# Gate and up projections by Strassen's seven products, with middle sums in PSUM

## The chip, the cores and the metric

The kernel runs on one core of a Trainium2 chip. The metric is device time in microseconds (us) of one execution. Engines are named as the profile names them: PE (TensorE, matrix products; PEld is its weight load), DVE (VectorE), ACT (ScalarE), POOL (GpSimd) and SP (SyncE, which issues DMAs).

## The reference

Two residual layers on x of 512 tokens by 1024 channels, float32. Layer 0 mixes tokens by chunked retention, layer 1 by stick-breaking attention. Each is followed by a feed-forward block, which is what the change is about:

```
h = rms_norm(x, ffn_norm)
gate, up = split(h @ w_in, 2)          # w_in: 1024 x 5632
x = x + (silu(gate) * up) @ w_out      # w_out: 2816 x 1024
```

## The kernel before

Everything is kept with channels on the partitions and the 512 tokens along the free dimension, so x is 8 tiles (k) of 128 channels by 512 tokens, and the 2816 hidden channels are 22 tiles (f).

**Float32 by three products.** PE works on float32r operands. Every operand is split in a high part and the float32r rest: weights by `Weights` (high `wh`, ACT, L72; rest `wl`, DVE, L73), activations by `to_pair`. `split3` (L131 to L133) then makes three matmuls for one product: high by high, high by low, low by high. Every matmul has its own weight load.

**Weights.** Each load is 128 by 1024 floats (512 KB), issued by SP in the order of use (L55), three ahead, in a ring of three `raw` buffers; the split is two ahead, in rings of three. One such item feeds 24 matmuls.

**Feed-forward** (`s_ffn`), once a layer:
- The norm's factor per token (`row`) comes late, from `stats_col` and `stats_row`, so the products run on x with the norm's gain only (`xh`, `xl`), and `ffn_act` multiplies gate and up by `row`.
- `ffn_first`: gate and up of f = 0, 1 in four banks, two k tiles a step, while the last tiles of x are finished.
- `ffn_tile(f)`: 24 matmuls of 512 columns for gate, 24 for up, a PSUM bank each. Then `ffn_act`: gate times `row` (L502, DVE), silu (L504, ACT), up times `row` (L506, DVE), product (L507, DVE), split into `hh` (L138, ACT) and `hl` (L139, DVE).
- After f = 10 and after f = 21 `ffn_out_chunk` multiplies the 11 hidden tiles by w_out, two output tiles at a time, and `add_x` (L233, DVE) adds the bank to x. The last output tile of the kernel is cut in two token halves of 256 columns, so that its first half leaves early; its adds are L526.

PSUM has eight banks in one ring (tag `mm`). The program is written as a list of steps; within an engine, the order of instructions that the queues finally hold is set at build time by a planner that takes the first instruction in program order whose operands it reckons ready. On the chip each engine runs its queue in that order and waits on semaphores.

Of the kernel before, what the change touches and what calls it, by code (L numbers as in the profile page):

```python
# [17 lines left out]
P = 128  # L18
# [8 lines left out]
HALF = FF // P // 2  # L27


class Weights:  # L30
    """Weights in the order of their use: loaded ahead, and split into a float32r
    part and the float32r rest, whose sum is the float32 weight."""

    def __init__(self, nc, raw, split, load_ahead, split_ahead):
        self.nc, self.raw, self.split = nc, raw, split
        self.aps, self.raws, self.parts = [], {}, {}
        self.n_load = self.n_split = self.n_take = 0
        self.load_ahead, self.split_ahead = load_ahead, split_ahead
        self.hooks = {}
        self.first = None  # per half of the first load: what to load before it, what to do before its split  # L40

    def load(self, n):
        nc = self.nc
        while self.n_load < min(n + self.load_ahead, len(self.aps)):
            for hook in self.hooks.pop(self.n_load, ()):
                hook()
            ap = self.aps[self.n_load]
            t = self.raw.tile([P, 1024], F32, tag="raw", name=f"raw{self.n_load}")
            w = ap.shape[-1]
            if self.n_load == 0 and self.first:  # L50
                for half, (ready, _) in zip((slice(0, w // 2), slice(w // 2, w)), self.first):
                    ready()
                    nc.sync.dma_start(t[:, half], ap[:, half])
            else:
                nc.sync.dma_start(t[:, :w], ap)  # L55
            self.raws[self.n_load] = (t, w)
            self.n_load += 1

    def advance(self, n):
        nc = self.nc  # L60
        self.load(n)
        while self.n_split < min(n + self.split_ahead, self.n_load):
            t, w = self.raws.pop(self.n_split)
            h = self.split.tile([P, 1024], F32R, tag="wh", name=f"wh{self.n_split}")
            l = self.split.tile([P, 1024], F32R, tag="wl", name=f"wl{self.n_split}")
            parts = [slice(0, w)]
            if self.n_split == 0 and self.first:
                parts = [slice(0, w // 2), slice(w // 2, w)]
            for i, part in enumerate(parts):
                if len(parts) > 1:  # L70
                    self.first[i][1]()
                nc.scalar.activation(h[:, part], t[:, part], AF.Copy)  # L72
                nc.vector.tensor_tensor(l[:, part], t[:, part], h[:, part].bitcast(F32), ALU.subtract)  # L73
            self.parts[self.n_split] = (h, l, w)
            self.n_split += 1

    def take(self):
        n = self.n_take
        self.advance(n + 1)
        self.n_take += 1  # L80
        return self.parts.pop(n)
# [3 lines left out]
def trunk(ctx, tc, x_in, gains_in, ret_tok, ret_ch, ret_o, sb_in, sb_o4, sb_o2, ffn_in2, ffn_in, ffn_out,  # L85
          cos_in, sin_in, decay_in, out):
    nc = tc.nc
    cp = ctx.enter_context(tc.tile_pool(name="cp", bufs=1))
    xp = ctx.enter_context(tc.tile_pool(name="xp", bufs=1))
    xgp = ctx.enter_context(tc.tile_pool(name="xgp", bufs=8))  # L90
    raw = ctx.enter_context(tc.tile_pool(name="raw", bufs=3))
    split = ctx.enter_context(tc.tile_pool(name="split", bufs=3))
    st = ctx.enter_context(tc.tile_pool(name="st", bufs=2))
    W = Weights(nc, raw, split, 3, 2)
    psr = ctx.enter_context(tc.tile_pool(name="psr", bufs=8, space=bass.MemoryType.PSUM))

    # gains: columns 0-15 mixer (layer, k), 16-31 ffn, 32-47 retention output, 48 q, 49 k
# [22 lines left out]
    zero = cp.tile([P, P], F32, name="zero")  # L120
    nc.vector.memset(zero, 0.0)
    start = psr.tile([P, S], F32, tag="mm", name="start")
# [5 lines left out]
    def split3(ps, a, b, start, stop):  # L128
        """(ah + al) b's three leading products; a and b are (high, low) pairs."""
# [5 lines left out]
    def to_pair(h, l, src, scale=None):  # L135
        """h + l = src * scale, both float32r."""
# [7 lines left out]
    def norm_in(k, gcol):  # L144
        """x[k] with the norm's gain (the norm's factor per token comes later), and its squares."""
# [35 lines left out]
    def tok_chunk(c, banks, kks=(0, 1)):  # L181
        """A quarter of [512 tokens, 512 outputs]: two k tiles."""
# [12 lines left out]
    def ch_tile(bank):  # L195
        """[128 outputs, 512 tokens]"""
# [6 lines left out]
    def ch_chunk(c, banks):  # L203
        """A quarter of four times [128 outputs, 512 tokens]: two k tiles."""
# [42 lines left out]
    def run():  # L247
        W.aps = list(order)
        W.hooks = load_hooks
        W.n_load = W.n_split = W.n_take = 0  # L250
        for fn in steps:
            fn()
        assert W.n_take == len(order)
        order.clear()
        steps.clear()

# [13 lines left out]

    def psum():
        return psr.tile([P, S], F32, tag="mm", name="mm")
# [19 lines left out]
    def rope_tables():  # L292
        # the norm's factor per token goes with the rotation
# [176 lines left out]
    ff = {}  # L470

    def ffn_open():
        ff["ctx"] = ExitStack()
        ff["p"] = ff["ctx"].enter_context(tc.tile_pool(name="ffp", bufs=HALF + 2))
        ff["t"] = ff["ctx"].enter_context(tc.tile_pool(name="fft", bufs=2))

    def ffn_first(c):
        def go():
            if c == 0:
                ff["first"] = [psum() for _ in range(4)]  # L480
            ch_chunk(c, ff["first"])
            if c == 3:
                stats_col(psum)
        return go

    def ffn_tile(f):
        def go():
            gate, up = psum(), psum()
            ch_tile(gate)
            if f == 2:  # L490
                stats_row(psum, ff["t"])
                ffn_act(0, *ff["first"][0:2])
            ch_tile(up)
            if f == 2:
                ffn_act(1, *ff["first"][2:4])
            ffn_act(f, gate, up)
        return go

    def ffn_act(f, gate, up):
        row = state["row"]  # L500
        gs = ff["t"].tile([P, S], F32, tag="gs", name="gs")
        nc.vector.tensor_tensor(gs, gate, row, ALU.mult)  # L502
        sil = ff["t"].tile([P, S], F32, tag="sil", name="sil")
        nc.scalar.activation(sil, gs, AF.Silu)  # L504
        us = ff["t"].tile([P, S], F32, tag="us", name="us")
        nc.vector.tensor_tensor(us, up, row, ALU.mult)  # L506
        nc.vector.tensor_tensor(us, us, sil, ALU.mult)  # L507
        h = ff["p"].tile([P, S], F32R, tag="hh", name="hh")
        l = ff["p"].tile([P, S], F32R, tag="hl", name="hl")
        to_pair(h, l, us)  # L510
        ff["hid"][f] = (h, l)

    def ffn_out_chunk(half, mp, c, gcol, to):
        cuts = [slice(0, S // 2), slice(S // 2, S)] if half == 1 and mp == 3 and to is out else []

        def go():
            if c == 0:
                ff["banks"] = [psum() for _ in range(2 + (len(cuts) > 0))]
            ks = list(range(4 * c, min(4 * c + 4, HALF)))
            out_chunk(ff["banks"], [ff["hid"][half * HALF + k] for k in ks], c == 0, c == 2, cuts=cuts)  # L520
            if c == 2:
                for m in range(2):
                    if cuts and m == 1:
                        for bank, cut in zip(ff["banks"][1:], cuts):
                            part = x[KT - 1][:, cut]
                            nc.vector.tensor_tensor(part, bank[:, : S // 2], part, ALU.add)  # L526
                            nc.sync.dma_start(to[KT - 1][:, cut], part)
                    elif half == 0:
                        add_x(2 * mp + m, ff["banks"][m], None)
                    else:  # L530
                        add_x(2 * mp + m, ff["banks"][m], gcol, to)
        return go

    def s_ffn(layer, gcol, to):
        step(ffn_open)
        ff["hid"] = {}
        for half in range(2):
            if half == 0:
                for c in range(4):
                    step(ffn_first(c), ffn_in2[layer, c])  # L540
            for f in range(2 if half == 0 else HALF, (half + 1) * HALF):
                step(ffn_tile(f), ffn_in[layer, f], ffn_in[layer, 2 * HALF + f])
            for mp in range(4):
                for c in range(3):
                    w = ffn_out[layer, half, mp][:, 1024 * c : min(1024 * (c + 1), 256 * HALF)]
                    step(ffn_out_chunk(half, mp, c, gcol, to), w)
        step(lambda: ff["ctx"].close())
# [347 lines left out]
```

## Time and profile before

| | |
|---|---|
| median of 3 runs | 1412.11 us (1411.46 to 1412.31) |
| span of the profiled execution, first to last instruction | 1412.2 us |
| PE busy | 1400.5 us, 99% |
| DVE, ACT, POOL busy | 736.5, 512.4, 205.8 us |
| bytes moved by DMA | 130.57 MB, 92 GB/s |

The profiled execution's span and the median of the runs are the same to 0.1 us, so times of the trace can be set against the median as they stand. "Busy" PE is a sum over overlapping matmuls; how fast PE goes is read from the distance between the starts of two matmuls.

### The profile page before, as it was taken

The page shows a single profiled execution, that of the slowest core. Times are in us where ns is not written, and L with a number is a line of the kernel's source. Part 1 is how long each engine was busy: PE and PEld are TensorE (multiplying, and loading weights), DVE is VectorE, ACT ScalarE, POOL GpSimd, SP SyncE. Part 2 cuts the span into 40 slices and gives each one's busy share as a digit, 9 for nine tenths or more (in the row PEclk, how much of TensorE's full clock was granted, in tenths as well). Part 3 has the DMA queues.
Part 4 walks back from the last instruction along what each step waited for, and adds up shares of the span by engine and source line. Part 5 has one row for each costly group of instructions (what it writes and reads, how often), then busy time and mean ns, then how long its engine had stood idle before and what let it go on. Part 6 is the DMA issues. An engine that isn't in the chain of part 4 may idle for free.

```text
span 1412.2 us, 16105 instructions
## 1 busy us (share of the span) xinstructions
PE 1400.5 (99%) x6331; PEld 1148.8 (81%) x6331; DVE 736.5 (52%) x947; ACT 512.4 (36%) x768; POOL 205.8 (15%) x262
## 2 busy tenths in 40 slices
PE   9999999999999999999999999999999999999999
PEld 7888888888888888888888877777788888888887
DVE  6555355364374443344434367889994443344432
ACT  5333233232353232223233356657653232223221
POOL 3000000000020000000002245677740000000000
PEclk9999999999999999999999999999999999999999
DMA  6332322213222323332334222122113323333232
GB/s 224 94 93 76 96 75 86 94 60 104 75 90 90 104 87 97 101 102 92 92 106 148 87 90 75 46 60 90 46 60 105 97 94 97 101 95 99 89 109 71
DMA packets 39388, 130.57 MB, mean 92 GB/s; under 512 B 4496, under 2 KB 4752, under 8 KB 39312
## 3 DMA queue, kind: packets, MB, share of 16 engines
q1 hardware_dynamic: 39312, 129.54, 29.6%
q8 instruction: 49, 0.80, 0.2%
q14 instruction: 27, 0.22, 0.0%
HBM read 125.33 MB, written 4.19 MB: 92 GB/s over the span
## 4 chain that ended last, share of the span: by engine, by line
PE 88%; DVE 4%; POOL 4%; issue 3%; ACT 1%; DMA 0%; POOLq 0%; SPq 0%; DVEq 0%; ACTq 0%
PE mm L131 29%; PE mm L133 29%; PE mm L132 28%; POOL w L667 1%; DVE sn L666 1%; POOL sn L660 1%; POOL w L660 1%; POOL qf L603 1%; PE mm L405 0%; DVE kk L636 0%; DVE wtl L139 0%; PE mm L701 0%; DVE wl L73 0%; PE mm L653 0%; PE mm L652 0%
## 5 line engine op out<-in xcount | busy, mean ns | idle before, releaser
L72 ACT ACTIVATE wh<-raw 128x1024 fp32r<-128x1024 f32 (+2 forms) x233 | 243.0, 1043 | 708.8 <-PE mm L132 413.2
L73 DVE TENSOR_TENSOR wl<-raw,wh 128x1024 fp32r<-128x1024 f32 (+2 forms) x233 | 286.2, 1229 | 276.6 <-ACT wh L72 275.5
L131 PE MATMUL mm<-xh,wh 128*128 128x512 f32 x832 | 324.5, 390 | 0.0
L133 PE MATMUL mm<-xh,wl 128*128 128x512 f32 x832 | 323.9, 389 | 0.0
L132 PE MATMUL mm<-xl,wh 128*128 128x512 f32 x832 | 323.8, 389 | 0.0
L132 PEld LDWEIGHTS mm<-xl,wh 128*128 128x128 f32 x832 | 156.2, 188 | 32.6
L133 PEld LDWEIGHTS mm<-xh,wl 128*128 128x128 f32 x832 | 156.2, 188 | 32.5
L131 PEld LDWEIGHTS mm<-xh,wh 128*128 128x128 f32 x832 | 156.2, 188 | 32.1
L132 PE MATMUL mm<-wl,xh 128*128 128x512 f32 x448 | 176.5, 394 | 1.9 <-DVE wl L73 1.9
L131 PE MATMUL mm<-wh,xh 128*128 128x512 f32 x448 | 176.8, 397 | 0.2 <-ACT wh L72 0.2
L133 PE MATMUL mm<-wh,xl 128*128 128x512 f32 x448 | 176.2, 393 | 0.0
L131 PE MATMUL mm<-hh,wh 128*128 128x512 f32 (+1 forms) x363 | 140.6, 387 | 0.0
L133 PE MATMUL mm<-hh,wl 128*128 128x512 f32 (+1 forms) x363 | 139.8, 385 | 0.0
L132 PE MATMUL mm<-hl,wh 128*128 128x512 f32 (+1 forms) x363 | 138.6, 382 | 0.0
L132 PEld LDWEIGHTS mm<-wl,xh 128*128 128x128 f32 x448 | 84.7, 189 | 20.0 <-DVE wl L73 2.6
L131 PEld LDWEIGHTS mm<-wh,xh 128*128 128x128 f32 x448 | 84.5, 189 | 19.6 <-issue 1.7
L158 POOL TENSOR_TENSOR sq<-sq,sqt 128x512 f32<-128x512 f32 x28 | 42.8, 1528 | 390.6 <-issue 293.9
L133 PEld LDWEIGHTS mm<-wh,xl 128*128 128x128 f32 x448 | 84.7, 189 | 18.1 <-issue 0.2
L506 DVE TENSOR_TENSOR us<-mm,row 128x512 f32<-128x512 f32 x44 | 30.4, 690 | 125.2 <-PE mm L133 125.2
L233 DVE TENSOR_TENSOR x<-mm,x 128x512 f32<-128x512 f32 x87 | 59.4, 686 | 57.6 <-PE mm L133 57.5
L133 PEld LDWEIGHTS mm<-hh,wl 128*128 128x128 f32 x363 | 68.1, 188 | 15.0
L132 PEld LDWEIGHTS mm<-hl,wh 128*128 128x128 f32 x363 | 68.1, 188 | 14.3
(115 smaller groups left out, 1608.2 us busy)
## 6 DMA issues: line engine op xcount, KB each, us to landing
raw<-in_ffn_in_dram SPq DMA_DIRECT2D x88, 512.0 KB, 3.5
raw<-in_ffn_out_dram SPq DMA_DIRECT2D x32, 512.0 KB, 3.6
raw<-in_ret_tok_dram SPq DMA_DIRECT2D x31, 512.0 KB, 3.6
raw<-in_sb_in_dram SPq DMA_DIRECT2D x24, 512.0 KB, 3.5
raw<-in_ret_ch_dram SPq DMA_DIRECT2D x16, 512.0 KB, 3.5
raw<-in_ret_o_dram SPq DMA_DIRECT2D x16, 512.0 KB, 3.5
raw<-in_ffn_out_dram SPq DMA_DIRECT2D x16, 384.0 KB, 3.1
raw<-in_sb_o_dram SPq DMA_DIRECT2D x8, 512.0 KB, 3.6
```

Of the source, the lines that this page charges most:

```text
L72: nc.scalar.activation(h[:, part], t[:, part], AF.Copy)
L73: nc.vector.tensor_tensor(l[:, part], t[:, part], h[:, part].bitcast(F32), ALU.subtract)
L131: nc.tensor.matmul(ps, ah, bh, start=start, stop=False)
L132: nc.tensor.matmul(ps, ah, bl, start=False, stop=False)
L133: nc.tensor.matmul(ps, al, bh, start=False, stop=stop)
L158: nc.gpsimd.tensor_tensor(state["sq"], state["sq"], t, ALU.add)
L233: nc.vector.tensor_tensor(x[m], bank, x[m], ALU.add)
L506: nc.vector.tensor_tensor(us, up, row, ALU.mult)
L603: nc.gpsimd.tensor_tensor(QF[which, g][:, t], ss, mhalf, ALU.pow)
L660: nc.gpsimd.affine_select(out=t[:, ts], in_=t[:, ts], compare_op=ALU.is_gt, fill=fill, base=0, pattern=[[-1, P]], channel_multiplier=1)
L666: nc.vector.tensor_tensor_scan(d, d, d, 1.0, ALU.mult, ALU.bypass)
L667: nc.gpsimd.tensor_tensor(w[:, 0 : n - 1], w[:, 0 : n - 1], r[:, 1:n], ALU.mult)
```

## The change

The two f tiles of a group, two token halves of 256 and pairs of k tiles are taken as 2 by 2 blocks, and the gate and up of the group's blocks come from seven block products instead of eight. f = 0 and 1 are left as they were; f = 2 to 21 are ten groups a layer.

- **Weights.** A group takes seven weight operands of 512 KB: `b11`, `b22` and `b21` as loaded, `t3` and `t1`, each a plain load by SP and a second load added onto it by an accumulating DMA issued by POOL, and `t2` and `t4`, sums on DVE. All seven are split in high and rest. The group's five raw tiles live in a ring of six. High parts are made up to four items ahead (before: three, in a ring of three; now a ring of four), sums up to five.
- **Activations.** `ffn_sums`, once for each pair of k tiles in `ffn_first`: the gained x again (two ACT), four sums of 256 columns (DVE), and their split (one ACT, one DVE of 1024 columns).
- **Products.** `product` is 24 matmuls of 256 columns, the two halves of one bank. Partial sums stay in PSUM: ACT copies bank a to bank b, later products accumulate on what was copied, ACT copies the second product to `p7`, and DVE adds `p7` twice.
- **Activation.** `row` multiplies the gate only; up's factor is applied to the output (`ffn_add`: two DVE instructions for an output tile where there was one).
- **Passes.** The output projection comes in three passes (8, 8 and 6 hidden tiles) in place of two of 11.
- **PSUM.** Two rings of four banks (`mm`, `sd`) in place of one of eight.

```diff
+PASSES = [range(0, 8), range(8, 16), range(16, FT)]
...
+    RAWS, GROUP_RAWS = 3, 6
...
+    def add(self, entry):
...
+            w11, w21, w12, w22 = entry
+            b11 = load(pos, w11)
+            t3 = load(pos + 1, w22, w12)
+            t1 = load(pos + 2, w11, w12)
+            b22 = load(pos + 2, w22)
+            b21 = load(pos + 3, w21)
+            t2, t4 = ("sum", pos + 2), ("sum", pos + 5)
+            self.items += [(b11, None), (t3, None), (t2, (t1, b22)), (b21, None), (t1, None), (t4, (t2, b21)),
+                           (b22, None)]
...
+                nc.sync.dma_start(t[:, :w], aps[0])
+                for ap in aps[1:]:
+                    nc.gpsimd.dma_start(t[:, :w], ap, accum_op=ALU.add)
...
+                t = self.group_pool.tile([P, 1024], F32, tag="sum", name="sum", bufs=3)
+                self.nc.vector.tensor_tensor(t, a, b, ALU.add)
...
     def take(self):
         n = self.n_take
-        self.advance(n + 1)
+        self.load(n + 1)
+        self.sum_to(n + 5)
+        self.high_to(n + 4)
+        self.low_to(n + 3)
...
+    def ffn_sums(p, layer):
+        xg = W.group_pool.tile([P, 2, S], F32, tag="sum", name="xg", bufs=3)
+        for i in range(2):
...
+            nc.scalar.activation(xg[:, i], x[k], AF.Copy, scale=gains[:, c : c + 1])
+        x21, x11, x22, x12 = xg[:, 0, H2], xg[:, 0, H1], xg[:, 1, H2], xg[:, 1, H1]
+        t = W.group_pool.tile([P, 4, S // 2], F32, tag="sum", name="xsum", bufs=3)
+        nc.vector.tensor_tensor(t[:, 0], x22, x21, ALU.subtract)
+        nc.vector.tensor_tensor(t[:, 1], x11, x21, ALU.subtract)
+        nc.vector.scalar_tensor_tensor(t[:, 2], t[:, 0], -1.0, x11, ALU.mult, ALU.subtract)
+        nc.vector.scalar_tensor_tensor(t[:, 3], x12, -1.0, t[:, 2], ALU.mult, ALU.subtract)
...
+        to_pair(h, l, t)
...
+    def product(bank, name, start):
+        h, l, _ = W.take()
...
+        for p in range(KT // 2):
+            xh, xl = ff["ops"][p][name]
+            for s in range(2):
+                out = bank[:, s * (S // 2) : (s + 1) * (S // 2)]
...
+                nc.tensor.matmul(out, h[:, p, s], xh, start=start and p == 0 and s == 0, stop=False,
+                                 skip_group_check=True)
+                nc.tensor.matmul(out, h[:, p, s], xl, start=False, stop=False, skip_group_check=True)
+                nc.tensor.matmul(out, l[:, p, s], xh, start=False, stop=last, skip_group_check=True)
...
+    def ffn_gate(src, half):
...
+        nc.scalar.activation(gs, gs, AF.Silu)
...
+    def ffn_up(f, src, gs, half):
...
+            nc.vector.scalar_tensor_tensor(us, src, -1.0, gs, ALU.mult, ALU.mult)
+            to_pair(h[:, :, half], l[:, :, half], halves(us))
+
+    def ffn_group(f, n):
...
+            if n == 0:
+                g["a"] = bank("mm")
+                product(g["a"], "11", True)
+                if f == 2:
+                    stats_row(lambda: bank("mm"), ff["t"])
+                    for i in range(2):
+                        ffn_up(i, ff["first"][2 * i + 1], ffn_gate(ff["first"][2 * i], None), None)
+                g["b"] = bank("sd")
+                nc.scalar.activation(g["b"], g["a"], AF.Copy)
+            elif n == 1:
+                t = bank("mm")
+                product(t, "s3", True)
+                g["p7"] = ff["t"].tile([P, S], F32, tag="p7", name="p7")
+                nc.scalar.activation(g["p7"], t, AF.Copy)
+            elif n == 2:
+                product(g["b"], "s2", False)
+                g["c"] = bank("sd")
+                nc.vector.tensor_tensor(g["c"], g["b"], g["p7"], ALU.add)
+            elif n == 3:
+                product(g["a"], "12", False)
+                g["gate"] = ffn_gate(g["a"], H1)
+            elif n == 4:
+                product(g["b"], "s1", False)
+                g["up"] = ff["t"].tile([P, S], F32, tag="up", name="up")
+                nc.vector.tensor_tensor(g["up"], g["b"], g["p7"], ALU.add)
+            elif n == 5:
+                product(g["c"], "22", False)
+                ffn_up(f, g["up"], ffn_gate(g["c"], H2), H2)
+            else:
+                product(g["b"], "s4", False)
+                ffn_up(f, g["b"], g["gate"], H1)
...
+    def ffn_add(m, src, cut, gcol, to):
+        t = ff["t"].tile([P, S], F32, tag="us", name="ty")
+        nc.vector.tensor_tensor(t[:, cut], src, state["row"][:, cut], ALU.mult)
+        nc.vector.tensor_tensor(x[m][:, cut], t[:, cut], x[m][:, cut], ALU.add)
```

## Rows read from the trace of the kernel before

**Rows 1.** The page's head, PE's busy time, granted TensorE clock in 40 slices

```profile
span 1412.2 us, 16105 instructions
PE 1400.5 (99%) x6331; PEld 1148.8 (81%) x6331; DVE 736.5 (52%) x947; ACT 512.4 (36%) x768; POOL 205.8 (15%) x262
PEclk9999999999999999999999999999999999999999
```

**Rows 2.** The chain that ended last, shares of the span by engine

```profile
PE 88%; DVE 4%; POOL 4%; issue 3%; ACT 1%; DMA 0%; POOLq 0%; SPq 0%; DVEq 0%; ACTq 0%
```

**Rows 3.** Busy time of each engine in three stretches, by window

```profile
core 0: us, PE busy (x) PEld busy (x) DVE busy (x) ACT busy (x) POOL busy (x), PEclk, DMA share, GB/s
411.00:772.00 361.00, 361.00 (x1594) 298.05 (x1593) 156.55 (x183) 106.65 (x130) 12.10 (x8) 1.00 0.33 101
842.00:1048.00 206.00, 200.66 (x953) 155.11 (x952) 181.59 (x260) 132.17 (x267) 134.85 (x195) 0.99 0.20 61
1048.00:1410.00 362.00, 361.10 (x1626) 299.32 (x1624) 154.03 (x179) 98.15 (x117) 7.81 (x5) 1.00 0.31 95
```

**Rows 4.** PE's timeline in a gate tile: start us, us, instruction

```profile
487.69 0.39 PE L131 MATMUL mm<-xh,wh 128*128 128x512 f32 x1
...
493.81 0.39 PE L131 MATMUL mm<-xh,wh 128*128 128x512 f32 x1
```

**Rows 5.** PE's timeline in the last output tile's first half

```profile
1396.33 0.28 PE L131 MATMUL mm<-hh,wh 128*128 128x256 f32 x1
...
1399.16 0.40 PE L131 MATMUL mm<-hh,wh 128*128 128x512 f32 x1
```

**Rows 6.** Groups by line: busy us, mean ns of one, idle before

```profile
L73 DVE TENSOR_TENSOR wl<-raw,wh 128x1024 fp32r<-128x1024 f32 (+2 forms) x233 | 286.2, 1229 | 276.6 <-ACT wh L72 275.5
L72 ACT ACTIVATE wh<-raw 128x1024 fp32r<-128x1024 f32 (+2 forms) x233 | 243.0, 1043 | 708.8 <-PE mm L132 413.2 <-issue 153.2 <-PE mm L133 142.3
L233 DVE TENSOR_TENSOR x<-mm,x 128x512 f32<-128x512 f32 x87 | 59.4, 686 | 57.6 <-PE mm L133 57.5
L502 DVE TENSOR_TENSOR gs<-mm,row 128x512 f32<-128x512 f32 x44 | 30.4, 690 | 81.6 <-PE mm L133 81.4
L139 DVE TENSOR_TENSOR hl<-us,hh 128x512 fp32r<-128x512 f32 x44 | 30.2, 686 | 4.2 <-ACT hh L138 4.2
L138 ACT ACTIVATE hh<-us 128x512 fp32r<-128x512 f32 x44 | 27.8, 632 | 33.5 <-DVE us L507 33.5
L504 ACT ACTIVATE sil<-gs 128x512 f32<-128x512 f32 x44 | 27.1, 617 | 2.6 <-DVE gs L502 2.5
L178 ACT ACTIVATE row<-mm 128x512 f32<-128x512 f32 x3 | 1.7, 578 | 0.0
```

**Rows 7.** DVE's timeline where nothing waits

```profile
456.73 0.69 DVE L507 TENSOR_TENSOR us<-us,sil 128x512 f32<-128x512 f32 x1
457.33 1.22 DVE L73 TENSOR_TENSOR wl<-raw,wh 128x1024 fp32r<-128x1024 f32 x1
458.47 0.68 DVE L139 TENSOR_TENSOR hl<-us,hh 128x512 fp32r<-128x512 f32 x1
```

**Rows 8.** DMA issues: KB each, median us from issue to landing

```profile
raw<-in_ffn_in_dram SPq DMA_DIRECT2D x88, 512.0 KB, 3.5
x<-x_kept SPq DMA_DIRECT2D x8, 256.0 KB, 4.5
```

**Rows 9.** POOL's timeline where layer 0's feed-forward begins

```profile
433.76 1.95 POOL L168 TENSOR_TENSOR rstd<-ms,mhalf 128x4 f32<-128x4 f32 x1 [16.93 <-DVE ms L166]
```

**Rows 10.** POOL's timeline at the kernel's start

```profile
12.35 7.09 POOL L158 TENSOR_TENSOR sq<-sq,sqt 128x512 f32<-128x512 f32 x4 [0.21 <-ACT sqt L157]
```

**Rows 11.** DVE's timeline at the kernel's start

```profile
12.62 2.30 DVE L73 TENSOR_TENSOR wl<-raw,wh 128x1024 fp32r<-128x1024 f32 x1
```

**Rows 12.** ACT's timeline after layer 1's first gate tile

```profile
1076.64 1.28 ACT L504 ACT_TABLE_LOAD   x1
```

**Rows 13.** DVE's timeline at the kernel's end

```profile
1409.14 0.42 DVE L526 TENSOR_TENSOR x<-mm,x 128x256 f32<-128x256 f32 x1 [0.64 <-PE mm L133]
```

More of the change, by code (lines that the diff above doesn't have):

```diff
@@ L39, in __init__, with load @@
         self.hooks = {}
         self.first = None
+        self.group_pool = None
+        self.loads, self.items = [], []
+        self.tiles, self.uses = {}, {}
+        self.ring = [[], []]
+        self.n_load = self.n_sum = self.n_h = self.n_l = self.n_take = 0
+        self.h, self.l = {}, {}
+    def add(self, entry):
+        pos = len(self.items)
+        def load(at, *aps):
+            self.loads.append((aps, isinstance(entry, tuple), at))
+            return ("load", len(self.loads) - 1)
+        if not isinstance(entry, tuple):
+            self.items.append((load(pos, entry), None))
+        else:
[8 more added lines that the diff above has]
+                           (b22, None)]
+        for src, parts in self.items[pos:]:
+            for name in (src, *(parts or ())):
+                self.uses[name] = self.uses.get(name, 0) + 1
@@ L42, in load, with use @@
+    def use(self, name):
+        t = self.tiles[name]
+        self.uses[name] -= 1
+        if not self.uses[name]:
+            del self.tiles[name]
+        return t
     def load(self, n):
         nc = self.nc
-        while self.n_load < min(n + self.load_ahead, len(self.aps)):
+        while self.n_load < len(self.loads):
+            aps, group, at = self.loads[self.n_load]
+            if group and self.group_pool is None:
+                return
+            bufs = self.GROUP_RAWS if group else self.RAWS
+            ring = self.ring[group]
+            if len(ring) >= bufs and ring[-bufs] in self.tiles:
+                return
+            if at >= n + (12 if group else self.load_ahead):
+                return
@@ L52, in load @@
                     ready()
-                    nc.sync.dma_start(t[:, half], ap[:, half])
+                    nc.sync.dma_start(t[:, half], aps[0][:, half])
             else:
-                nc.sync.dma_start(t[:, :w], ap)
-            self.raws[self.n_load] = (t, w)
-            self.n_load += 1
-    def advance(self, n):
-        nc = self.nc
[L61 to L75, printed above, removed]
+                nc.sync.dma_start(t[:, :w], aps[0])
@@ new lines, in load, with sum_to @@
+                for ap in aps[1:]:
+                    nc.gpsimd.dma_start(t[:, :w], ap, accum_op=ALU.add)
+            self.tiles["load", self.n_load] = (t, w)
+            self.ring[group].append(("load", self.n_load))
+            self.n_load += 1
+    def sum_to(self, n):
+        while self.n_sum < min(n, len(self.items)):
+            src, parts = self.items[self.n_sum]
+            if parts:
+                if any(name not in self.tiles for name in parts):
+                    return
+                (a, w), (b, _) = (self.use(name) for name in parts)
+                t = self.group_pool.tile([P, 1024], F32, tag="sum", name="sum", bufs=3)
+                self.nc.vector.tensor_tensor(t, a, b, ALU.add)
+                self.tiles[src] = (t, w)
+            self.n_sum += 1
@@ L478, in go, with ffn_first @@
+    def ffn_first(c, layer):
         def go():
             if c == 0:
-                ff["first"] = [psum() for _ in range(4)]
+                ff["first"] = [bank("sd") for _ in range(4)]
             ch_chunk(c, ff["first"])
+            ffn_sums(c, layer)
             if c == 3:
-                stats_col(psum)
+                stats_col(lambda: bank("mm"))
         return go
-    def ffn_tile(f):
-        def go():
[L488 to L496, printed above, removed]
-        return go
@@ L499, in ffn_act @@
[L499 to L511, printed above, removed]
@@ L516, in go @@
         def go():
             if c == 0:
[L518 to L531, printed above, removed]
+                ff["banks"] = [bank("mm") for _ in range(2 + (len(cuts) > 0))]
@@ new lines, in go @@
+            tiles = [[t[:, f % 2] for t in ff["hid"][f // 2]] for f in fs[4 * c : 4 * c + 4]]
+            out_chunk(ff["banks"], tiles, c == 0, c == n - 1, cuts=cuts)
+            if c < n - 1:
+                return
+            whole = slice(0, S)
+            for m in range(2):
+                if cuts and m == 1:
+                    for src, cut in zip(ff["banks"][1:], cuts):
+                        ffn_add(KT - 1, src[:, : S // 2], cut, None, to)
+                else:
+                    ffn_add(2 * mp + m, ff["banks"][m], whole, gcol if last else None, to if last else None)
@@ L535, in s_ffn @@
         step(ffn_open)
[L536 to L542, printed above, removed]
+        step(lambda: ff.update(hid={}))
+        for c in range(4):
+            step(ffn_first(c, layer), ffn_in2[layer, c])
+        f = 2
+        for i, fs in enumerate(PASSES):
+            while f <= fs[-1]:
+                blocks = tuple(ffn_in[layer, f // 2 - 1, k, j] for j in range(2) for k in range(2))
+                for n in range(7):
+                    step(ffn_group(f, n), *([blocks] if n == 0 else []))
+                f += 2
+            w = ffn_out[i][layer]
+            n = -(-len(fs) // 4)
             for mp in range(4):
[L544 to L547, printed above, removed]
+                for c in range(n):
+                    step(ffn_out_chunk(fs, mp, c, n, gcol, to), w[mp][:, 1024 * c : min(1024 * (c + 1), 256 * len(fs))])
+        step(ffn_close)
     s_ffn(0, 8, x_kept)
```

136 lines of the change are left out of this document (107 added, 29 removed).

## The prediction

> **What bounds the kernel now.** I read the page's first part, then the chain, then the windows by stage, then single timelines. [...] Busy alone proves little, since matmuls overlap, but the chain that ended last is PE for 88% of the span too [rows 2]. The two feed-forward blocks are the stretches 411 to 772 us and 1048 to 1410 us, 361 and 362 us, half of the kernel. There PE never rests, DVE is busy 156.6 of 361 us (43%), ACT 30%, and the DMA engines 33% [rows 3]. So here time is the number of matmuls times their pace, and DVE, ACT and DMA have room. What the change asks is how much of that room it eats for how many matmuls.
>
> The pace is the distance of starts. Twenty-seven intervals of 512-column matmuls in a gate tile take 493.81 - 487.69 = 6.12 us, 0.2267 us each [rows 4]. The kernel also holds the shape that the change uses, 256 columns with a weight load each: 24 of them, between the first of the half tile and the next full-width one, take 1399.16 - 1396.33 = 2.83 us, 0.1179 us each [rows 5]. Half the columns cost 52% of the time.
>
> **What PE saves.** A group of two f tiles was four tiles of 24 matmuls: 96 x 0.2267 = 21.76 us. It becomes seven products of 24: 168 x 0.1179 = 19.81 us. Strassen's eighth (12.5%) shrinks to 9%. Twenty groups (ten a layer): 20 x 1.95 = **39 us**. Bounds: 256 columns at exactly half of 0.2267 would give 20 x (21.76 - 19.04) = 54 us; at 0.1295 us a matmul (21.76 / 168) it would give nothing. I take 0.1179, the same instruction form in the same program. The output projection keeps its 528 matmuls a layer, in three passes in place of two.
>
> [...]
>
> **What DVE gets.** Per group, with durations of [rows 6]: rests of weights, 7 for 4, at 1.23 us; two weight sums of the same 1024 columns, which I price alike; and eight 512-column instructions at 0.69 us (two adds of `p7`, two gate products, two up products, two rests), as many as before, since up's `row` factor has left. Total 9 x 1.23 + 8 x 0.69 = 16.6 us for 19.8 us of PE: 84%. Where nothing waits, instructions start closer than they last, 0.60 us apart for 512 columns and 1.14 for 1024 [rows 7]; by that it is 9 x 1.14 + 8 x 0.60 = 15.1 us, 76%. ACT: 7 x 1.04 + 6 x 0.63 = 11.1 us, 56%. Neither is the bound by sum, but DVE's 43% is nearly doubled.
>
> **What now waits for whom.** Before, no matmul of a tile needed a result of DVE or ACT but its split weights. Now four handoffs a group go PE to ACT or DVE and back to PE. Each is covered by one product in between, 24 x 0.118 = 2.83 us: the copy a to b is covered by the second product, the copy to `p7` and the first add by the fourth, the second add by the sixth. The worst that should stand before each in its queue is one weight instruction: on ACT 1.04 + 0.58 (a copy out of PSUM, L178) = 1.6 us, on DVE 1.23 + 0.69 = 1.9 us, plus some 0.2 us for each semaphore, all below 2.83. Cost from below nothing; from above, if the cover is gone, the whole saving of 1.95 us a group. What takes the cover away is DVE's order: behind the last two products stand chains DVE, ACT, DVE (gate, silu, up, high, rest), in which DVE stands for some 0.8 us at each of three ACT steps unless the planned order has a weight instruction there: 2.4 us a group, 16.6 + 2.4 = 19.0 us against 19.8. I take 0.4 us a group, near the lower end because the covers hold singly and 0.8 us remain even with every wait counted: **+8 us**.
>
> **DMA.** Loads go from four to seven a group, two of them accumulating, which no row of this trace shows. Price: below, a plain load of 3.5 us; above, two plain loads and the longest POOL instruction near, 2 x 3.5 + 1.95 = 9.0 us [rows 8, 9]; the nearest row is the reload of x, which also follows a wait on data, at 4.5 us for half the bytes. I take 3.5 + 1.95 = 5.5 us. Behind its base load that is 9 us (12.5 at most). A ring place for `t1` comes free when the `t3` before it is split, at the latest in the product before a group; its sum is needed in the ninth product after, less 3.5 us of sum and split: 9 x 2.83 - 3.5 = 22 us. That hides it. In volume: 0.33 x 361 us for 101 GB/s x 361 us / 0.524 MB = 70 loads is 1.7 us of all DMA engines a load; 7 x 1.7 = 12 us a group, 19 if an accumulate costs three loads, below 19.8. So nothing on the path, but SP and POOL now wait in line: POOL's second load waits for SP's first to land, and behind it only the next accumulate stands, except at the ends of a block, where POOL also squares and sums x.
>
> **Where a block starts and ends.** `ffn_sums` adds per k pair two ACT and five DVE instructions; by 4 x 0.42 + 1.23 = 2.9 us [rows 6, 13] on DVE and 2 x 0.63 + 1.04 = 2.3 on ACT, beside 24 x 0.2267 = 5.4 us of PE: hidden; without that cover 12 us a layer. In the first group, bank b is a place that f = 0's gate must leave first: `row` (0.58), gate (0.69), silu (0.62), copy (0.62), with semaphores 3 us against 2.83, in layer 1 with a table load of 1.28 us more [rows 12]; PE may take the fourth product meanwhile. I take 1 us a layer, **+2** (bounds 0 and 8). The kernel's last half tile gets a second DVE instruction of 0.42 us [rows 13]: **+0.4**. The 32 more DVE instructions a layer in the output passes (22 us) lie beside matmul time of 11 us for two tiles, where DVE has some 5 us to do. The two rings of four banks leave the other stages as they were as long as `psum` alternates; the earlier high parts ask nothing of PE. Nothing each, within 3 us.
>
> **Sum.** 1412.2 (the profiled execution, 0.1 above the median) - 39.1 + 8 + 2 + 0.4 = **1383.5 us**.
>
> **Rivals.**
> - *DVE becomes the bound (slower).* At the kernel's start, while POOL adds squares, each 1.77 us of a queue without pause [rows 10], the rest of a weight tile takes 2.30 us instead of 1.23 [rows 11, 6]. If POOL's work for two accumulating DMAs slows DVE like that, 1.5 tiles each, a group's DVE work is 19.0 + 3 x 1.07 = 22.2, and with 0.8 us of waits for PE's handoffs 23.0 us: 20 x (23.0 - 21.76) + 2.4 = +27, **1439 us**. It decides from 21.64 us a group on. For it: DVE at 84%, in-order queues, and the mixing stretch 842 to 1048 us, where DVE at 88% already holds PE up. Against: what POOL does for a DMA is not a sum over tiles, and no row shows it. [...]
> - *Late sums.* The order was laid out with some assumed time for an accumulating DMA. If the real one is nearer 9 us, DVE stands at `t2`'s sum, what hands off to PE stands behind it, and PE loses about 1.2 us a group, 24 us: **1408 us** by 1383.5 + 24. A little more and nothing is left, 1409 to 1415.
> - *The products don't run at 0.118 us.* Twice the instructions per time, seven times as long as the half tile's stretch of 24. At 0.1295 us PE saves nothing: **1422 us** with the other terms. Against it: the rate is even over all the rows of that form.
>
> **How the numbers follow.** A change under 0.2% (2.8 us) can't be told from none. Main case, stalls of 0 to 1.1 us a group: 0.58, 1371 to 1398. Better than that (faster pace, no stalls): 0.04. Late sums with a rest of the gain, 1398 to 1409: 0.10. Gain all eaten, 1409 to 1415: 0.06. Slower, by DVE (0.18) or pace (0.04): 0.22, half of it below 1425. Faster 0.72, same 0.06, slower 0.22. The range 1371 to 1425 leaves out 0.04 below and about 0.11 above; the likeliest case's own range is 1371 to 1398.
>
> **What would show it.** Right: starts of 256-column matmuls 0.118 us apart through a group, a block of about 347 us in place of 361, DVE near 80% busy there, wl still 1.23 us, and few waits of PE on DVE. Wrong: wl of 1.5 us and more beside POOL, PE waiting for DVE's adds or for wl in each group, DVE waiting for a DMA before its sums, or blocks as long as before.

## The result and the profile after

The changed kernel takes **1474.97 us** (median of 4 runs, 1472.98 to 1479.06) against 1412.21 (1411.46 to 1414.24) on the same chip: ratio **1.0444**, 95% interval 1.0426 to 1.0462. It is slower by 63 us, where I forecast 29 us faster; it lies above the whole range. The profiled execution spans 1477.3 us, and the rows below are of it. It is the longest of the four, 1479.06 us by the metric. In every recorded run the metric is some 1.7 us above the span, so that the span before (1412.2) agrees with its median only by chance, and the spans differ by 65.1 us where the medians differ by 62.8.

The page's head, PE's busy time, the granted clock in 40 slices and the chain, as in [rows 1, 2]:

```profile
span 1477.3 us, 19590 instructions
PE 1396.2 (95%) x7756; PEld 1213.4 (82%) x7756; DVE 902.6 (61%) x1148; ACT 611.6 (41%) x892; POOL 241.4 (16%) x302
...
PEclk8999999999998999999999999989999999989999
...
PE 19%; DMA 3%; DVE 1%; issue 0%; DVEq 0%; SPq 0%
```

PE is busy for 95% where it was 99%. The chain holds only 23% of the span, so it says little here, but DMA and DVE stand in it beside PE. The waits, by engine and line (us in total, times, longest), say more:

```profile
PE mm L610 <- DVE mm L672: 37.6, 15, 3.8
PE mm L268 <- POOL rstd L261: 11.8, 2, 9.0
PE mm L224 <- ACT wh L147: 9.4, 1, 9.4
DVE sum L121 <- DMA rawg<-in_ffn_in_dram: 82.8, 18, 7.2
```

PE waits 15 times, 2.5 us each on average, for the add that makes `c` (L672); in the first block of the kernel before PE waited for DVE nowhere. And VectorE stands 18 times before a sum of weights (L121) until a load lands, 17 of them before `t2`. The same pair is seen in one group. VectorE's timeline (start us, us, instruction, idle before and its releaser):

```profile
1252.31 1.22 DVE L150 TENSOR_TENSOR wl<-rawg,wh 128x1024 fp32r<-128x1024 f32 x1
...
1260.32 1.23 DVE L150 TENSOR_TENSOR wl<-rawg,wh 128x1024 fp32r<-128x1024 f32 x1 [1.00 <-PE mm L613]
1267.26 1.22 DVE L121 TENSOR_TENSOR sum<-rawg 128x1024 f32<-128x1024 f32 x1 [5.72 <-DMA rawg<-in_ffn_in_dram]
1268.40 0.69 DVE L672 TENSOR_TENSOR mm<-mm,p 128x512 f32<-128x512 f32 x1
```

The loads behind it, on SP's and POOL's timelines and, last, the DMA issues of the stretch 1258.7 to 1259.5 us alone (KB, us to landing):

```profile
1253.56 0.33 SPq L106 DMA_DIRECT2D rawg<-in_ffn_in_dram  x1
1256.39 0.86 POOL L108 DMA_DIRECT2D rawg<-in_ffn_in_dram  x1 [19.00 <-DVE hl L232]
1258.47 0.86 POOL L108 DMA_DIRECT2D rawg<-in_ffn_in_dram  x1 [1.21 <-DMA rawg<-in_ffn_in_dram]
...
rawg<-in_ffn_in_dram POOLq DMA_DIRECT2D x1, 512.0 KB, 8.8
rawg<-in_ffn_in_dram SPq DMA_DIRECT2D x1, 512.0 KB, 7.6
```

And PE around it:

```profile
1262.76 0.28 PE L613 MATMUL mm<-sxh,wl 128*128 128x256 f32 x1
...
1263.84 0.28 PE L613 MATMUL mm<-xh,wl 128*128 128x256 f32 x1
...
1265.64 0.28 PE L613 MATMUL mm<-xh,wl 128*128 128x256 f32 x1
1269.15 0.38 PE L610 MATMUL mm<-sxh,wh 128*128 128x256 f32 x1 [3.23 <-DVE mm L672]
...
1270.23 0.41 PE L612 MATMUL mm<-sxl,wh 128*128 128x256 f32 x1
...
1273.21 0.32 PE L610 MATMUL mm<-sxh,wh 128*128 128x256 f32 x1
```

This is one stall from end to end. The rest `wl` at 1252.31 ends at 1253.53 and frees a ring place; SP starts `t1`'s base load into it at 1253.56; POOL adds the second block from 1258.47 on, and that lands 8.8 us later, at 1267.27. The sum `t2 = t1 + b22` of the *next* group starts at 1267.26. Six products lie before the one that uses it, but it stands in VectorE's queue ahead of `c`, whose own inputs were there at about 1263.0, the end of the third product (its last matmul is the first row of PE above). The fifth product adds to the bank that `c` reads, so PE waits 3.23 us.

The accumulating load is not alone in it. The sum's other input, `b22`, is a plain load into the next place that comes free; SP issued it at 1258.74, and beside the accumulating loads it took 7.6 us, to 1266.37. Of the 17 waits before `t2` it landed last in nine, by 0.2 to 1.5 us, and the accumulating load in eight.

Then comes a second price. Fifteen intervals before the stall take 1265.64 - 1263.84 = 1.80 us, 0.120 us each. Shortly after it, 14 intervals from 1270.23 to 1273.21 take 2.98 us, 0.213 us each. The granted clock of that stretch is 0.50 in place of 1.00; over the whole kernel the granted share shows 8 in places where [rows 1] have 9 throughout. That costs 14 x 0.093 = 1.3 us more. Not every stall has this second price: after the one that ended at 1155.54 (3.00 us) the clock stayed at 1.00. By window, columns as in [rows 3]:

```profile
1155.60:1158.60 3.00, 3.00 (x26) 3.00 (x27) 3.00 (x4) 0.23 (x1) 0.00 (x0) 1.00 0.02 5
1270.20:1273.20 3.00, 3.00 (x16) 3.00 (x15) 2.88 (x4) 0.63 (x1) 0.00 (x0) 0.50 0.00 0
```

In the whole trace nine of the 15 stalls are followed by 13 to 27 matmuls at this pace, 1.2 to 2.6 us each, 16.4 us in all; the other six by none.

Busy time in the two feed-forward blocks and between, columns as in [rows 3]:

```profile
412.00:785.00 373.00, 347.27 (x2282) 321.61 (x2281) 232.71 (x271) 150.62 (x187) 25.30 (x26) 0.96 0.48 134
785.00:1060.00 275.00, 262.32 (x1186) 204.86 (x1185) 204.11 (x291) 153.99 (x293) 151.40 (x203) 0.96 0.23 75
1060.00:1477.00 417.00, 385.60 (x2473) 353.08 (x2471) 266.60 (x315) 163.91 (x207) 37.16 (x41) 0.96 0.45 125
```

The granted clock is 0.96 where it was 1.00 or 0.99. PE's timeline gives the borders of the stages (the first matmul of each; the last stage runs to the end of the span), in us:

| stretch | before | after | difference |
|---|---|---|---|
| start to first feed-forward | 410.7 | 418.9 | +8.2 |
| feed-forward, layer 0 | 361.8 | 381.2 | +19.4 |
| output, mixing of layer 1 | 274.5 | 288.4 | +13.9 |
| feed-forward, layer 1 | 365.3 | 388.9 | +23.6 |

Outside the blocks, the first product of the kernel waited, on ACT's and PE's timelines:

```profile
15.01 1.13 ACT L147 ACTIVATE wh<-raw 128x512 fp32r<-128x512 f32 x2
...
15.68 0.80 PE L224 MATMUL mm<-wh,xh 128*128 128x512 f32 x1 [9.43 <-ACT wh L147]
```

Items one and two have their high parts on ACT (10.86 and 14.07 us) ahead of the first item's.

And at the head of a block PE waits up to 9.0 us for `rstd`. DVE's and POOL's timelines there:

```profile
450.13 0.15 DVE L259 TENSOR_SCALAR ms<-mm 128x4 f32<-128x4 f32 x1
...
451.56 0.87 POOL L108 DMA_DIRECT2D rawg<-in_ffn_in_dram  x1 [6.35 <-DVE wl L150]
452.13 1.36 POOL L261 TENSOR_TENSOR rstd<-ms,mhalf 128x4 f32<-128x4 f32 x1
```

### The profile page after: what moved, and what is told of

It is laid out like the page before. It is cut to its first block, busy times and chain, and to the rows that moved or that the text cites. A ratio compares the mean times of both kernels' runs of the same rounds, so it can differ in the third digit from the quotient of the medians.

```text
span 1477.3 us, 19590 instructions
## 1 busy us (share of the span) xinstructions
PE 1396.2 (95%) x7756; PEld 1213.4 (82%) x7756; DVE 902.6 (61%) x1148; ACT 611.6 (41%) x892; POOL 241.4 (16%) x302
## 5 line engine op out<-in xcount | busy, mean ns | idle before, releaser
L133 ACT ACTIVATE wh<-raw 128x1024 fp32r<-128x1024 f32 (+1 forms) x151 | 156.7, 1037 | 369.6 <-PE mm L225 180.8
L150 DVE TENSOR_TENSOR wl<-raw,wh 128x1024 fp32r<-128x1024 f32 (+1 forms) x151 | 186.7, 1239 | 174.4 <-PE mm L225 93.5
L610 PE MATMUL mm<-sxh,wh 128*128 128x256 f32 x640 | 190.5, 298 | 37.6 <-DVE mm L672 37.6
L612 PE MATMUL mm<-sxl,wh 128*128 128x256 f32 x640 | 187.5, 293 | 0.0
L613 PE MATMUL mm<-sxh,wl 128*128 128x256 f32 x640 | 187.2, 293 | 0.0
L610 PEld LDWEIGHTS mm<-sxh,wh 128*128 128x128 f32 x640 | 129.7, 203 | 40.8 <-DVE mm L672 40.6
L610 PE MATMUL mm<-xh,wh 128*128 128x256 f32 x480 | 136.5, 284 | 0.0
L613 PE MATMUL mm<-xh,wl 128*128 128x256 f32 x480 | 136.2, 284 | 0.0
L612 PE MATMUL mm<-xl,wh 128*128 128x256 f32 x480 | 136.1, 283 | 0.0
L613 PEld LDWEIGHTS mm<-sxh,wl 128*128 128x128 f32 x640 | 129.6, 202 | 0.0
```

The lines of the kernel that those rows point to most:

```text
L133: self.nc.scalar.activation(h[:, :w], t[:, :w], AF.Copy)
L150: nc.vector.tensor_tensor(l[:, :w], t[:, :w], h[:, :w].bitcast(F32), ALU.subtract)
L610: nc.tensor.matmul(out, h[:, p, s], xh, start=start and p == 0 and s == 0, stop=False, skip_group_check=True)
L612: nc.tensor.matmul(out, h[:, p, s], xl, start=False, stop=False, skip_group_check=True)
L613: nc.tensor.matmul(out, l[:, p, s], xh, start=False, stop=last, skip_group_check=True)
```

## The experiments

My theory at this point: the sum's place in VectorE's queue, together with the landing of the accumulating load, makes the stalls; three other things cost the rest (the first high part, POOL's queue at `rstd`, the two PSUM rings).

**Hold the sum to its place** (`pin_sums`), the changed kernel with

```
-                self.nc.vector.tensor_tensor(t, a, b, ALU.add)
+                self.tc.keep_in_program_order(self.nc.vector.tensor_tensor(t, a, b, ALU.add))
```

> Only DVE's order is changed: each weight sum stays behind everything that comes before it in the program, so that it no longer stands ahead of the first add of p7. Theory (PE waits for that add because the add stands behind a sum that waits for a load): the 15 waits of PE on the add (38 us idle) and most of the half-rate stretches behind them (about 20 us) go; 1412 to 1422 us, a group in steady state at 20 to 21 us. Rival (DVE has too much work, or the handoffs themselves are too slow): the waits move to another DVE instruction and the time stays within 10 us of 1475.

1424.35 us, 2 us above the range; ratio to before, on the same chip here and below, 1.0073 (1.0045 to 1.0100). VectorE now, in the same place of another group:

```profile
1209.86 0.70 DVE L673 TENSOR_TENSOR mm<-mm,p 128x512 f32<-128x512 f32 x1 [1.60 <-PE mm L614]
...
1215.50 0.69 DVE L680 TENSOR_TENSOR up<-mm,p 128x512 f32<-128x512 f32 x1 [1.01 <-PE mm L614]
1216.11 1.22 DVE L121 TENSOR_TENSOR sum<-rawg 128x1024 f32<-128x1024 f32 x1
```

The sum stands behind `up`, two products later, and waits for nothing. PE's wait for `c` is gone. The blocks are 354.8 and 359.1 us: 56.2 us less in the two. Of these PE's waits were 37.6; of the remaining 18.6 the nine half-rate stretches make 16.4. From the start of one group to the next it is 20.0 us in every place but the first group of a layer (31.6 and 27.6); in the changed kernel it was 20.0 to 26.6.

**No accumulating loads** (`no_second`): the line `nc.gpsimd.dma_start(t[:, :w], ap, accum_op=ALU.add)` is left out with its loop, so `t3` and `t1` hold one block each.

> Left out: the second, accumulating load of t3 and t1, so that those two operands are one block instead of a sum. Order and every wait but those on POOL's loads stay. Theory that the accumulating loads make the waits (8.5 us to landing, and the plain load beside them 6 us instead of 3.6): the waits on the first add fall from about 3.3 us to under 1 us a group, 1415 to 1430 us; POOL's rstd is no longer late either (12 us). Rival (the plain load that is issued last is late by itself): PE still waits 2 us or more a group, 1445 us or more.

1408.57 us, ratio 0.9967 (0.9955 to 0.9980), 6 us below the theory's range, with the sum still ahead of `c` in VectorE's queue. The sum's waits:

```profile
DVE sum L119 <- DMA rawg<-in_ffn_in_dram: 13.9, 19, 1.0
```

19 waits of 0.7 us on average in place of 18 of 4.6. The blocks are 344.0 and 355.3 us. So both halves are needed for the stall: the early place and the slow landing. The second half is the landing of both inputs: here, with no accumulating load beside it, `b22` lands in 3.3 to 3.7 us in all groups but the first of a layer. Here even the first groups are short, 20.8 and 22.3 us.

**One place more in the ring** (`raws7`): does the place come free too late, or is the order laid out with too short a landing? `GROUP_RAWS` 6 to 7, and the high parts as in the kernel before, one `wh` buffer of 128 by 1024 given up for the place:

```
-    RAWS, GROUP_RAWS = 3, 6
+    RAWS, GROUP_RAWS = 3, 7
...
-            h = self.split.tile([P, 1024], F32R, tag="wh", name=f"wh{self.n_h}", bufs=4)
+            h = self.split.tile([P, 1024], F32R, tag="wh", name=f"wh{self.n_h}", bufs=3)
...
-        self.high_to(n + 4)
+        self.high_to(n + 3)
```

> The changed kernel with seven places for loads in place of six (for which there is space only with three high parts, three ahead); the sums stand where the planner puts them, ahead of the add c. If the stall comes from a ring place that comes free too late, a load can start one use earlier, the sum's data are there in time and most of the 14 to 15 stalls go: about 1430 us. If it comes from the planner, which reckons with a shorter landing than the accumulating load takes and moves the sum earlier by as much as the loads gain, the groups stay at 24 to 27 us and the time near 1470.

1482.36 us, ratio 1.0502 (1.0485 to 1.0519). Its waits of PE and DVE:

```profile
PE mm L613 <- DVE wl L150: 36.9, 13, 3.7
...
DVE sum L121 <- DMA rawg<-in_ffn_in_dram: 112.1, 36, 6.4
```

Twice as many sums wait, and PE loses the same 37 us, now at weights that stand behind the sum. With the loads earlier the order put the sums earlier too: in a group under way `t1`'s base load starts 3.2 us before the group's first matmul (0.8 in the changed kernel), and VectorE stands at `t2`'s sum from 3.8 us after it (7.2). The three high parts are not the cause: in `wh3` below, with three, such groups take 20.0 us. One more buffer did not mend an order that counts on data too soon.

**Also the first high part** (`mend`): `pin_sums`, and at the first `take`

```
+        if n == 0:
+            self.sum_to(1)
+            self.high_to(1)
+            self.low_to(1)
```

> As the first of these runs, and the first weight tile's high part is put ahead of the next three again. Theory: the first product starts at about 6.5 us as before instead of 15.7, and the whole is 8 us under the first of these runs, 1404 to 1414 us. Rival (what the start loses is won back while the loads catch up): less than 2 us of difference.

1414.31 us, ratio 1.0008 (0.9996 to 1.0020): no faster than the kernel before. The first feed-forward starts at 411.7 us, after 418.5 in `pin_sums`.

**Two rings in the kernel before** (`before_rings`):

```
-    psr = ctx.enter_context(tc.tile_pool(name="psr", bufs=8, space=bass.MemoryType.PSUM))
+    psr = ctx.enter_context(tc.tile_pool(name="psr", bufs=4, space=bass.MemoryType.PSUM))
+    turn = [0]
...
-        return psr.tile([P, S], F32, tag="mm", name="mm")
+        turn[0] += 1
+        return psr.tile([P, S], F32, tag=("mm", "sd")[turn[0] % 2], name="mm")
```

> The kernel before with its PSUM banks in two rings of four, taken in turn, and nothing else. If the rings are what makes the mixing stretch of layer 1 14 us longer: 1422 to 1428 us. If they do nothing there: 1410 to 1415 us.

1421.46 us, ratio 1.0055 (1.0040 to 1.0070), at the lower end of the theory's range. The stretch between the blocks is 281.5 us, 7.0 more, and nothing else moves. One wait of that stretch that the kernel before does not have to this length (0.3 us there):

```profile
PE mm L682 <- DVE qs L143: 3.5, 2, 2.5
```

**One ring in `mend`** (`one_ring`), **also fewer accumulating loads ahead of `rstd`** (`all3`), **also three high parts** (`all4`):

```
-    psr = ctx.enter_context(tc.tile_pool(name="psr", bufs=4, space=bass.MemoryType.PSUM))
+    psr = ctx.enter_context(tc.tile_pool(name="psr", bufs=8, space=bass.MemoryType.PSUM))
...
-        return psr.tile([P, S], F32, tag=tag, name="mm")
+        return psr.tile([P, S], F32, tag="mm", name="mm")
```

`all3` and `all4` also, with `stats` set once the block's statistics are issued:

```
-            if at >= n + (12 if group else self.load_ahead):
+            if at >= n + ((12 if self.stats else 8) if group else self.load_ahead):
...
-                    nc.gpsimd.dma_start(t[:, :w], ap, accum_op=ALU.add)
+                    self.tc.keep_in_program_order(nc.gpsimd.dma_start(t[:, :w], ap, accum_op=ALU.add))
```

and `all4` also has the two edits of `raws7` to the high parts.

These three change the middle sums in PSUM: with one ring, copies to which products are added land in other banks than before, and how that changes the sums no run isolates. All instructions and bytes are there, and only the times are read.

> The kernel of mend (t2's sum held to its place, the first high part first) with one PSUM ring of eight banks in place of two of four. The theory that the two rings hold up the mixing stretch: the stretch between the two feed-forwards falls from 285.9 us by about 7, as it rose by 7.0 when the kernel before was given two rings, and the wait of 2.6 us on x at the start of the second feed-forward goes; near 1405 us. The rival, that the mixing stretch is longer for the accumulating loads that start in it: within 2 us of mend's 1414.

> one_ring, and the accumulating loads started at most eight loads ahead until rstd is computed, and in program order on POOL, so that rstd has two of them ahead of it and not all that fit. The theory that POOL's queue makes PE wait for rstd: the waits of 8.5 and about 3 us at the start of the two feed-forwards go, and with them a stretch of PE at half rate after each; 1388 to 1395 us. The rival, that rstd is late for its own inputs: no different from one_ring, near 1405.

> all3 with the high parts three ahead and three buffers for them, as in the kernel before. If the fourth high part is what is left of the longer mixing stretch (about 4 us over the kernel before's 274.5): 3 to 5 us below all3. If it costs nothing: within 2 us of all3; and if it is needed to hide ScalarE's work at the group starts, the groups of 20.0 us get longer and the time is above all3's.

`one_ring` 1407.36 us (0.9964, 0.9950 to 0.9977), `all3` 1407.62 (0.9968, 0.9953 to 0.9982), `all4` 1398.97 (0.9901, 0.9888 to 0.9913). `one_ring` gained the 7 us expected, but its mixing stretch is only 2.9 us shorter, as far as one trace of each shows; the wait for x at the head of the second block went. `all4` gained twice what I expected of the high parts. `all3` met its rival: PE's waits for `rstd` stayed (15.4 us in two). Its rows of PE, DVE and POOL, in this order, show why:

```profile
433.16 0.95 PE L263 MATMUL mm<-ones,sq 128*128 128x1 f32 x8
444.55 1.12 PE L274 MATMUL mm<-ident,rstd 128*128 128x128 f32 x4 [7.46 <-POOL rstd L267]
...
430.00 1.23 DVE L122 TENSOR_TENSOR sum<-rawg 128x1024 f32<-128x1024 f32 x1 [6.96 <-DMA rawg<-in_ffn_in_dram]
...
442.31 0.15 DVE L265 TENSOR_SCALAR ms<-mm 128x4 f32<-128x4 f32 x1
...
442.55 1.95 POOL L267 TENSOR_TENSOR rstd<-ms,mhalf 128x4 f32<-128x4 f32 x1 [23.28 <-DVE ms L265]
```

POOL had been free for 23 us. The statistics' matmuls ended at 434.1, and `ms`, 0.15 us long, ran 8.2 us later, behind the token sums of the last k pairs, which VectorE reached late because it had stood 7 us before the block's first sum of weights. **My theory of POOL's queue fell**: it is the same stall once more, and the accumulate ahead of `rstd` in the changed kernel cost at most the 1.9 us between `ms` (450.28) and `rstd` (452.13).

**The statistics two chunks earlier** (`early_stats`), **three high parts in `mend`** (`wh3`, by the two edits of `raws7` to them), **both** (`best`), all on `mend` with its two rings. The edit of `early_stats`:

```
             ch_chunk(c, ff["first"])
+            if c == 1:
+                stats_col(lambda: bank("mm"))
             ffn_sums(c, layer)
-            if c == 3:
-                stats_col(lambda: bank("mm"))
```

> The kernel of mend with the statistics of the norm taken after the second of the four first chunks and not after the fourth, so that the scale ms stands in VectorE's queue right behind the first sum of weights and ahead of two rounds of token sums. The theory formed from the last runs (in all3 POOL was free 23 us before rstd and rstd waited for ms, which stood in VectorE's queue from the end of its matmuls at 434.1 us to 442.3): PE's waits of 8.5 and 2.6 us for rstd go, with the half-rate stretch behind each, 11 to 15 us below mend's 1414, near 1400. The rival, POOL's queue of accumulating loads: the accumulate that stood ahead of rstd is still there, the waits stay, within 3 us of mend.

> The kernel of mend with three high parts, three ahead, as in the kernel before (two PSUM rings kept). If the fourth high part lengthens the mixing stretch by itself: that stretch falls from 285.9 us to the 281.5 that two rings alone gave, about 4 us, near 1409. If it and the rings get in each other's way (all4 against all3 gave 12 us at one ring): 274 to 278 and 1400 to 1404.

> early_stats and wh3 together. If the two causes add: 11 to 15 us for the statistics and 4 to 12 for the fourth high part below mend's 1414, so 1387 to 1399, 1 to 1.8 per cent under the kernel before. If the groups need the fourth high part once PE no longer waits for rstd, the groups grow beyond 20.0 us and the time stays at 1400 or above.

`early_stats` 1407.17 us (0.9961, 0.9946 to 0.9976), `wh3` 1408.61 (0.9971, 0.9962 to 0.9981), `best` **1400.95** (0.9919, 0.9907 to 0.9930). `wh3` came out at the time forecast for a fourth part that costs by itself, but its trace does not show where: the stretch fell by 3.1 us, the first block grew by 3.1, and the two spans are the same to 0.2 us (1410.2 and 1410.0). `best` is 2 us above its forecast. In `early_stats`, DVE and then PE:

```profile
427.99 1.23 DVE L121 TENSOR_TENSOR sum<-rawg 128x1024 f32<-128x1024 f32 x1 [7.12 <-DMA rawg<-in_ffn_in_dram]
429.13 0.15 DVE L264 TENSOR_SCALAR ms<-mm 128x4 f32<-128x4 f32 x1
...
434.81 0.60 PE L273 MATMUL mm<-ident,rstd 128*128 128x128 f32 x4
...
443.26 0.58 PE L615 MATMUL mm<-sxh,wh 128*128 128x256 f32 x1 [3.16 <-ACT mm L668]
```

`ms` is right behind the sum, the transposes wait for nothing, and the blocks shrink by 3.0 and 4.9 us, to 351.4 and 353.4. That is less than the 11 to 15 forecast: 3.16 us come back at the next handoff, the copy of the first group's `a` to `b`, and the stretch between the blocks grew by 5.7 us to 291.6 for reasons that no run separates. The theory holds, its size was too large. `best` is faster than both kernels, by 0.8% than the one before (0.7 to 0.9) and by 5% than the changed one.

The stretch between the blocks, over all kernels: with three high parts and one ring 274.5 (before) and 274.2 (`all4`); with three and two rings 281.5 to 282.9 (`before_rings`, `raws7`, `wh3`, `best`); with four, 283.0 to 291.6 whatever the rings. So with three high parts the two rings cost 7 to 9 us; the fourth costs 3 to 12 by what stands beside it, and the two do not add. Each of these lengths is read from one execution, and the executions of one kernel differ by up to 9.5 us (`all3` 1403.86 to 1413.35), so a difference of 3 us here is not shown. How the rings do it, beyond the longer wait for `qs`, stays open.

## Why the prediction was wrong

**PE's saving: right.** A group takes 20.0 us where nothing stalls, 168 x 0.1190, against 21.76 before [rows 4]: 1.76 us each, 35 us in all, where I had 39. The four products on token sums run at 0.118 us a matmul, as in [rows 5], the three on x itself at 0.120; no run shows why. The rival in which the products run at 0.1295 us is refuted.

**"The worst that should stand before each in its queue is one weight instruction": the step that failed.** A second kind stood there, a sum that waits for a DMA. I priced the 1.23 us that it is busy and not the wait that it brings along. VectorE kept the order of its queue: `c`'s inputs were there at 1263.0, and `c` started at 1268.40, after the sum (1267.26). The 0.2 us for each semaphore were my estimate, above what the trace of the kernel before shows (0.08 us from `ms` to `rstd`, 0.15 from `oms` to `ors`), and played no part: `c` ends at 1269.09, and PE starts at 1269.15, 0.06 us later.

**"9 x 2.83 - 3.5 = 22 us. That hides it": wrong by the deadline.** The place came free in the product before the group, as I assumed (1253.5 us), and the load took 13.7 us to 1267.27, against my 9 (12.5 at most). But I counted to the sum's need, in the ninth product, where the queue sets another deadline: whatever stands behind the sum. That was `c`, whose inputs were there 9.5 us after the place came free. And I had reckoned with `t1` alone: `b22`'s place came free 5 us later, and its load, 3.5 us by itself, took 7.6. With the sum held behind `up` the stalls are gone, but the margin is small: in eight of the 20 groups of `pin_sums` the later of the two loads lands only 0.1 to 2.3 us before the sum.

**The term of +8 us for stalls measured 56.** The rival of late sums named the mechanism, at 1.2 us a group (24 us); it was 2.8 a group on average. Its size missed two things: the loads were later, and nine of the 15 stalls were followed by a stretch at half rate (16.4 of the 56.2 us; 37.6 are the waits themselves).

**The first groups: +2 (bounds 0 and 8) became 19.** 31.6 and 27.6 us in `pin_sums` in place of 20.0. `no_second`, where they are 20.8 and 22.3, shows that the price hangs on the accumulating loads; `early_stats` shows that part of it goes by way of `ms`. The path that I costed (row, gate, silu, copy) is what appears once `rstd` is out of the way: 3.16 us for the copy.

**"the earlier high parts ask nothing of PE" and the two rings "within 3 us": wrong.** The start costs 8.2 us; undoing it in `mend` gave 7 back. There I had looked at what the parts ask, and not at what they stand ahead of on ACT. The mixing stretch cost 13.9, by rings and high parts together (without accumulating loads, in `no_second`, the stretch is 288.5 us, as long as with them), and how they do it is open.

**DVE as the bound: refuted, though the sign of this rival came true.** In the changed kernel, in the groups by line, beside 40 accumulating loads:

```profile
L150 DVE TENSOR_TENSOR wl<-rawg,wh 128x1024 fp32r<-128x1024 f32 x100 | 121.9, 1219 | 44.6 <-PE mm L613 31.3
L108 POOL DMA_DIRECT2D rawg<-in_ffn_in_dram x40 | 34.9, 873 | 582.5 <-issue 200.9
```

A rest takes 1.22 us as before [rows 6], and a group without stalls is as long as its matmuls.

The sum closes, in us of the two profiled spans: start +8.2, mixing +13.9, sums +56.2, first groups +19.2, saving -35.2, and 2.8 that I don't assign: 65.1, which is 1477.3 - 1412.2. Without accumulating loads the two blocks take 699.3 us; by my terms (727.1 - 39.1 + 8 + 2 + 0.4) it would have been 698.4. That this agrees is partly luck: the groups of `no_second` have none of the 8 us of stalls, and the saving is 4 us smaller. Still the forecast of the blocks was for a kernel whose sums wait for next to nothing.

## What to carry to other kernels

When a change puts an instruction that waits for a DMA on an engine that also hands off to TensorE, look at what stands behind it in that queue: its deadline is theirs, not that of its own consumer (here `c`, with its inputs there at 1263.0 and started at 1268.40). One more buffer did not buy out an order that counted on its loads too soon (1482.36 us); holding the waiting instruction behind the handoffs did (1424.35). Count every input of that instruction, the plain loads beside the new kind too (`b22` landed last in nine of the 17 waits). A stall of TensorE can cost more than its length: here the half rate after nine of 15 added 16.4 us to 37.6, and the length of a stall alone did not tell which (2.46 us had it, 3.00 us had not).

## What the runs showed of the hardware

The DMA issues of the changed kernel (KB each, median us from issue to landing):

```profile
rawg<-in_ffn_in_dram SPq DMA_DIRECT2D x100, 512.0 KB, 4.6
raw<-in_ffn_out_dram SPq DMA_DIRECT2D x40, 512.0 KB, 3.7
rawg<-in_ffn_in_dram POOLq DMA_DIRECT2D x40, 512.0 KB, 6.8
```

An accumulating load of 512 KB takes 6.8 us at the median (5.2 to 12.8); the one of the stall above took 8.8, with another and two plain loads beside it. The plain loads become slower: 4.6 us at the median, against 3.5 in [rows 8] and the 3.6 that the same 100 loads take in `no_second`; the 61 that overlap an accumulating load take 5.9, the other 39 still 3.6. POOL is busy for 0.87 us with each accumulating load. After PE's idle stretch of 3.2 us the granted clock fell from 1.00 to 0.50; the matmuls show it from 0.9 us after the restart, and full pace again from 1273.4 us.
